# Weight sums of the first FFN moved to the first projection, and the context's gate and up as half-precision pairs

## The chip, the core and the metric

The kernel runs on one core of a Trainium2 chip. The metric is the device time of one execution, in microseconds. Five engines work beside each other, each through its own queue in order: TensorE (PE, with the weight load PEld beside it), VectorE (DVE), ScalarE (ACT), GpSimd (POOL) and SyncE (SP). SP, POOL and ACT can start transfers between HBM and SBUF.

## The reference

Two layers of a backbone over 1024 latent tokens and 256 context tokens, with 1024 channels. Layer 0 mixes with a Fourier part and a Hyena part (long convolutions), layer 1 with neighbourhood attention. Each layer ends with a SwiGLU block, which is what the change is about:

```python
def swiglu(u, w_gate, w_up, w_down):
    return (jax.nn.silu(u @ w_gate) * (u @ w_up)) @ w_down
...
        h_lat = h_lat + g2 * swiglu(modulate(rms_norm(h_lat, norm2_g[i]), sh2, sc2),
                                    ffn_w_gate[i], ffn_w_up[i], ffn_w_down[i])
        if not last:
            h_ctx = h_ctx + cg1 * y_ctx
            h_ctx = h_ctx + cg2 * swiglu(modulate(rms_norm(h_ctx, norm2_g[i]), csh2, csc2),
                                         ffn_w_gate[i], ffn_w_up[i], ffn_w_down[i])
```

The hidden width is 2816, which is 22 blocks of 128 columns; gate and up together are 44 weight tiles of 128 x 1024 floats (512 KB) for each layer. Inputs and outputs are float32.

## The kernel before, in words

**Two numbers for one.** A float32 operand is split into a high and a low part, and a product is three matmuls: high by high, high by low, low by high. There are two kinds of pair. `split` (L285) makes a pair of rounded float32 parts: ScalarE copies the high part (L287), VectorE subtracts (L289). `half_split` (L1215) makes a pair of float16 parts: ScalarE multiplies by a scale and rounds (L1218), VectorE forms the rest (L1219). The float16 pair needs a scale, so that its values fit: for weights it is taken from the sum of absolute values of the tiles (`abs_sums`, L1247; the instruction is on L1251), added over the partitions by a small matmul on TensorE (`over_partitions`, L1294) and inverted on VectorE (`scale_cols`, L1311); for activations it comes from the modulation columns (`operand_scale`, L1221, with an all-reduce on GpSimd). The result of a product is multiplied by the inverse of both scales.

**The stages that matter here, in order.**

- *First projection* (`in_proj`, L779): 16 output blocks over latent and context tokens. For each, ScalarE sums a weight tile three blocks ahead and splits the one of the next block; results are evicted by ScalarE and VectorE. Two generators run beside it, called once per block: the context's filter (`filter_raw`, `filter_spectrum`), whose eight matrices go through `cmat` (L321), and the modulation columns (`ada_group`).
- *First output projection* (`out_proj`, L1178): eight output blocks for the context and the first half of the latent tokens (`pcs` (2, 0)), then `after1`, then eight for the other half. Operands are float32 pairs. A generator, `qkv_sums` (L1253), is called once per block: it loads 44 weight tiles over the GpSimd queue and sums them on ScalarE, three to a call. Four of them are layer 0's first gate and up tiles, 32 are for attention, eight are for layer 1's gate and up.
- `after1` spills the new residual, normalizes the context into float32 pairs (`norm_block`, L537), computes the operand scale and the scales of the four early tiles (`first_scales`, L1269), and begins the latent operands (`wino_first`, L1321).
- *Context's gate and up* (first loop of `ffn`, L1491): for each of 22 blocks, two weight tiles are loaded over SP into an `s4` tile and split into float32 pairs; 48 matmuls of 128x256 follow (`lin`, L338), then Silu on ScalarE (L1529) and a product on VectorE (L1530). The pairs rotate over the tags `wh`, `wl` and, every third time, both buffers of `ws` (`pair3`, L301); the last two blocks use `wh` and `wl` alone.
- *Latent gate and up* (second loop of `ffn`): a Strassen-Winograd scheme on 512-token halves, 11 pairs of blocks, seven products each for gate and up, in float16 pairs (L1449); ScalarE snaps results out of PSUM (L1454). `wino_weights` (L1395) loads two tiles for a key, one into `ws` and one into `s4`, and, where the scale isn't there yet, sums both and makes it (`weight_scale`, L1305).
- Afterwards: the down projections, attention, and layer 1's FFN, which the diff doesn't touch.

**What sets the order.** The program is written against a tile framework. Each tag of a pool has a fixed number of buffers: `ws`, `wh` and `wl` have two each (pool `pw`, 128 x 1024 floats), `s4` has 20. The framework plans a timeline with a cost model at build time: on each engine the ready instruction that stands first in the program goes next, and a tile takes a buffer when one is free. So an instruction can go far ahead of its place in the program, as far as buffers allow; on the chip each engine then keeps that planned order, and waits at an instruction whose operand isn't there. `follow` (L226) ties instructions behind a given one. `ld` starts a transfer from SP, `ldr` from GpSimd, `lda` from ScalarE. `PAD_C` is an unused column block ahead of the constants.

Of the kernel before, what the change touches and what calls it, by code (L numbers as in the profile page):

```python
# [32 lines left out]
PAD_C, PAD_T, SHIFT = 176, 160, 16  # L33
# [168 lines left out]
class Builder:  # L202
# [176 lines left out]
    def weights16(self, src, scale, w=1024, cut=False, load=None):  # L379
        st = self.pw.tile([P, 1024], F32, tag="ws", name=self.nm("ws"))  # L380
        hi, lo = (self.pw.tile([P, 1024], F16, tag=g, name=self.nm(g)) for g in ("wh", "wl"))
        (load or self.ld)(st.rearrange("p (n k) -> p n k", n=4) if cut else st[:, :w], src)
        self.half_split(st[:, :w], scale, hi[:, :w], lo[:, :w])
        return hi, lo
# [830 lines left out]
    def half_split(self, src, scale, hi, lo):  # L1215

        nc = self.nc
        nc.scalar.activation(hi, src, AF.Copy, scale=scale)  # L1218
        nc.vector.scalar_tensor_tensor(lo, src, scale, hi, op0=MUL, op1=SUB)  # L1219
# [33 lines left out]
    def qkv_sums(self):  # L1253

        a = self.a
        self.qs = self.C(44)
        src = [a["wv"][ch, kp] for ch in range(2) for kp in range(4)]
        src += [a[n][b] for n in ("wq", "wk", "w_out2") for b in range(KB)]
        for l, i in ((0, 0), (1, 0), (1, 1)):
            src += [a[n][l, 2 * i + k] for n in ("gate", "up") for k in (0, 1)]  # L1260
        for j, k in enumerate((32, 33, 34, 35, *range(32), *range(36, 44))):
            t = self.S4()
            self.ldr(t, src[k])
            self.abs_sums([t], self.qs[:, k:k + 1])
            if j % 3 == 2:
                yield
        yield

    def first_scales(self, l):  # L1269

        keys = [(l, i, m) for i in range(l + 1) for m in (0, 1)]
        n, k = len(keys), 3 * len(self.wsc)
        q = self.qs[:, 32 + 4 * l:36 + 8 * l]
# [217 lines left out]
    def ffn(self, l, u, h, hs, second, after, keep=None, begun={}):  # L1491
# [28 lines left out]
        if u is not None:  # L1520
            for fb in range(NFB):
                wide = 3 if fb < NFB - 2 else 2
                gh, gl = self.weights(a["gate"][l, fb], wide=wide)
                uh, ul = self.weights(a["up"][l, fb], wide=wide)
# [4 lines left out]
                nc.scalar.activation(t[:, :256], ga[:, :256], AF.Silu)  # L1529
                nc.vector.tensor_tensor(t[:, :256], ua[:, :256], t[:, :256], MUL)  # L1530
# [591 lines left out]
    def run(self):  # L2122
# [100 lines left out]
        self.in_proj(u, ((filt, 1), (ada, 2)))  # L2223
# [59 lines left out]
        def after1(pcs):  # L2283
            spill(h, hs0, pcs)
            if 0 in pcs:
                uf.t.update(self.new_act(pcs=(2,)).t)
                rs = self.rms(pcs)
                for b in range(KB):
                    self.norm_block({b: h.ap(0, b, 2)}, b, 2, 0, 3, uf, rs[0])
                load_h((1,))  # L2290
                self.ucol, self.usi = self.operand_scale(0, 3, (0, 1))
                self.first_scales(0)
# [219 lines left out]
```

## Time and profile before

| | us |
|---|---|
| median of 3 runs | 2919.48 |
| lowest and highest | 2914.33, 2921.39 |
| the profiled execution | 2919.95 |
| its span, first to last instruction | 2918.2 |
| first projection, about | 200 to 405 |
| first output projection, about | 725 to 850 |
| context's gate and up, about | 850 to 981 |
| latent gate and up of layer 0, about | 981 to 1320 |

The profile is of one execution. Its page gives each engine's busy time, a table of 40 slices, the transfer queues, a chain of waits followed back from the end, and groups of instructions: line, engine, operation, output and input names, shape and count, busy time and mean, and then the idle time of the engine just before them with what ended it. In a timeline, a row is the start, the duration, the engine and the line; an idle time before it, and who ended it, stands in brackets. A stage row gives the stretch, its length, the busy time and count of PE, PEld, DVE, ACT and POOL, the granted TensorE clock (1.00 is full), the busy share of the transfer engines, and GB/s. Matmuls are pipelined, so the distance from one start to the next is the cost, not the duration.

### The profile page before, as it was taken

What the parts mean: (1) busy time and instruction counts of PE and PEld (TensorE: products, weight loads), DVE (VectorE), ACT (ScalarE), POOL (GpSimd) and SP (SyncE); (2) the same over time, 40 slices, a digit from 0 to 9 for tenths busy, and PEclk for the clock granted to TensorE, in tenths of its full rate; (3) what the DMA queues carried; (4) which work ended last, traced back from release to release, by engine and by line L of the source; (5) the groups of instructions that cost most, each with busy time, mean ns of one, the idle gap of its engine ahead of it and who ended that gap; (6) DMA issues with size and microseconds to landing.
All of it is one profiled execution on the core that took longest, in us unless ns stands there. A gap on an engine that the chain in (4) does not pass through costs nothing. (4 is left out here: it accounts for less than half of the span.)

```text
span 2918.2 us, 46050 instructions
## 1 busy us (share of the span) xinstructions
PE 2766.6 (95%) x16163; PEld 1714.2 (59%) x16163; DVE 2094.0 (72%) x3833; ACT 1647.7 (56%) x2899; POOL 642.6 (22%) x1057
## 2 busy tenths in 40 slices
PE   6989999999989999999999999999999999999998
PEld 3766557888879644444555844676665444444554
DVE  4778867585467798877886767776676778775765
ACT  4674324454675667654555555676664477654553
POOL 1012013354220121213120012444443022112000
PEclk8989999999999999999999999999999999999999
DMA  6574434358785555566994798777775666424753
GB/s 254 187 265 161 161 122 151 111 168 286 285 344 182 207 205 197 201 213 240 327 333 161 273 337 294 179 188 172 185 198 188 236 226 231 153 93 184 242 191 113
DMA packets 325156, 615.98 MB, mean 211 GB/s; under 512 B 90934, under 2 KB 130552, under 8 KB 324922
## 3 DMA queue, kind: packets, MB, share of 16 engines
q1 hardware_dynamic: 252378, 384.38, 39.9%
q0 software_dynamic: 70240, 224.45, 21.6%
q10 hardware_dynamic: 2304, 4.20, 0.4%
q8 instruction: 127, 2.08, 0.3%
q14 instruction: 107, 0.88, 0.1%
HBM read 455.33 MB, written 135.53 MB: 202 GB/s over the span
## 5 line engine op out<-in xcount | busy, mean ns | idle before, releaser
L1449 PE MATMUL ps<-s,s 128*128 128x512 f16 x2592 | 582.2, 382 | 14.4 <-ACT tk L1454 6.8
L1449 PEld LDWEIGHTS <-s 128*128 128x128 f16 x2640 | 259.0, 98 | 332.6 <-issue 27.8
L283 PE MATMUL ps<-s,wh 128*128 128x256 f32 (+3 forms) x1752 | 398.2, 331 | 11.1 <-ACT wh L287 5.4
L1218 ACT ACTIVATE s<-s,c 128x512 f16<-128x512 f32 (+1 forms) x324 | 233.5, 754 | 141.9 <-DMA s<-d 79.9
L1219 DVE SCALAR_TENSOR_TENSOR s<-s,c,s 128x512 f16<-128x512 f32 (+1 forms) x324 | 247.4, 794 | 84.5 <-ACT s L1218 84.1
L1666 PE MATMUL ps<-s 128*128 128x512 f16 (+2 forms) x1308 | 303.4, 378 | 2.0 <-DVE s L1219 2.0
L283 PE MATMUL pq<-s,wh 128*128 128x512 f16 (+1 forms) x1000 | 280.3, 354 | 9.8 <-DMA wh<-d 5.4
L283 PE MATMUL ps<-s,wl 128*128 128x256 f32 (+3 forms) x876 | 261.6, 331 | 1.3 <-DVE wl L289 1.2
L283 PEld LDWEIGHTS <-wh 128*128 128x128 f16 x1664 | 160.9, 99 | 170.2 <-issue 20.9
L1666 PEld LDWEIGHTS <-s 128*128 128x128 f16 x1536 | 148.5, 98 | 178.9 <-issue 6.5
L274 POOL DMA_DIRECT2D d<-s x201 | 109.0, 543 | 640.5 <-DVE s L1510 178.6
L283 PE MATMUL ps<-s,s 128*128 128x65 f16 (+5 forms) x2666 | 222.3, 236 | 27.5 <-DMA s<-s 11.4
L335 ACT CAST mat<-cs 128x1024 fp32r<-128x1024 f16 (+2 forms) x120 | 111.6, 935 | 140.6 <-PE ps L283 57.3
L283 PEld LDWEIGHTS ps<-s,wh 128*128 128x128 f32 x1088 | 177.5, 192 | 18.1 <-ACT wh L287 5.7
L283 PE MATMUL ps<-s,mat 128*128 128x512 f32 x696 | 184.7, 413 | 3.3 <-DVE s L289 2.9
L1449 PE MATMUL ps<-s,wh 128*128 128x512 f16 x616 | 184.9, 379 | 1.8 <-DVE g L1463 1.4
L283 PE MATMUL pq<-s,wl 128*128 128x512 f16 (+1 forms) x500 | 174.5, 354 | 0.5 <-DMA wl<-d 0.5
L283 PEld LDWEIGHTS <-s 128*128 128x128 f16 x2400 | 114.5, 98 | 82.9 <-DMA s<-s 11.5
L283 PEld LDWEIGHTS ps<-s,mat 128*128 128x128 f32 x696 | 136.5, 199 | 37.9 <-DVE s L289 3.8
L1251 ACT ACTIVATE t<-s 128x1024 bf16<-128x1024 f32 (+1 forms) x164 | 141.9, 867 | 12.2 <-DVE c L470 8.4
L283 PEld LDWEIGHTS ps<-s,s 128*128 128x128 f32 (+1 forms) x746 | 113.6, 192 | 32.1 <-ACT s L287 7.0
L283 PEld LDWEIGHTS <-wl 128*128 128x128 f16 x832 | 82.3, 99 | 77.4 <-issue 4.5
(431 smaller groups left out, 5477.3 us busy)
## 6 DMA issues: line engine op xcount, KB each, us to landing
s<-d SPq DMA_DIRECT2D x294, 256.0 KB, 4.0
d<-s POOLq DMA_DIRECT2D x157, 256.0 KB, 3.2
s<-in_down SPq DMA_DIRECT2D x154, 256.0 KB, 5.4
s<-in_ada_w POOLq DMA_DIRECT2D x48, 512.0 KB, 4.8
g<-in_bias POOLq DMA_DIRECT2D x128, 192.0 KB, 3.6
s<-in_gate SPq DMA_DIRECT2D x46, 512.0 KB, 3.7
s<-in_up SPq DMA_DIRECT2D x46, 512.0 KB, 4.0
d<-g POOLq DMA_DIRECT2D x87, 256.0 KB, 2.9
```

Of the source, the lines that this page charges most:

```text
L274: self.last_ldr = self.nc.gpsimd.dma_start(out, in_).ins
L283: self.nc.tensor.matmul(o, l, r, start=st, stop=sp)
L335: self.nc.scalar.copy(m, st)
L1218: nc.scalar.activation(hi, src, AF.Copy, scale=scale)
L1219: nc.vector.scalar_tensor_tensor(lo, src, scale, hi, op0=MUL, op1=SUB)
L1251: self.nc.scalar.activation(junk[:, :t.shape[1]], t, AF.Abs, scale=2.0 ** -15, accum_out=st[:, k:k + 1])
L1449: nc.tensor.matmul(ps, x[:, sl], y, start=first and j == 0 and x is wh and y is xh, stop=j == 3 and x is wl, skip_group_check=True)
L1666: m = nc.tensor.matmul(acc[j][:, c0:c1], x[:, sl], y[:, xs], start=first and k == 0, stop=last and k == 2, skip_group_check=True)
```

## The change

Four things are changed.

1. **Sums of all 44 gate and up tiles of layer 0 ahead of the FFN.** A new generator `gate_sums` loads 32 of them over ScalarE's own queue into the two `ws` buffers and sums them in place on ScalarE: two loads ahead of the first projection, then two sums, each followed by the next load, at each of its 16 blocks. The other 12 go to the head of `qkv_sums`, which then has 52 tiles: four to a call for the first 16, then three.
2. `first_scales(0)` makes all 22 scales of layer 0 at once, from the new columns `fs`. `wino_weights` then finds every scale of layer 0 and sums nothing. Layer 1 is unchanged.
3. **The context's gate and up use float16 pairs.** The context is normalized after the operand scale is there, with `norm_half` in place of `norm_block`; the weights come from a new function `weights3`, which keeps the rotation over `wh`, `wl` and `ws` for all 22 blocks; the inverse scales go into the Silu and into the product.
4. `PAD_C` falls by 40 columns and `qs` by 4, against 44 columns for `fs`.

```diff
--- before.py
+++ after.py
@@ -30,7 +30,7 @@
 WID = {0: 512, 1: 512, 2: 256, 3: 256, 4: 256}
 OFF = {0: 0, 1: 512, 3: 512, 4: 768}
 KSTART = (0, 8, 24, 32)
-PAD_C, PAD_T, SHIFT = 176, 160, 16
+PAD_C, PAD_T, SHIFT = 136, 160, 16
 BOPS = ("B11", "B21", "T2", "T1", "T3", "B22", "T4")
 
 
@@ -381,6 +381,15 @@
         hi, lo = (self.pw.tile([P, 1024], F16, tag=g, name=self.nm(g)) for g in ("wh", "wl"))
         (load or self.ld)(st.rearrange("p (n k) -> p n k", n=4) if cut else st[:, :w], src)
         self.half_split(st[:, :w], scale, hi[:, :w], lo[:, :w])
+        return hi, lo
+
+    def weights3(self, src, scale):
+        self.p3 = (getattr(self, "p3", 0) + 1) % 3
+        tags = ("ws", "ws") if self.p3 == 0 else ("wh", "wl")
+        st = self.S4()
+        hi, lo = (self.pw.tile([P, 1024], F16, tag=g, name=self.nm(n)) for g, n in zip(tags, ("wh", "wl")))
+        self.ld(st, src)
+        self.half_split(st, scale, hi, lo)
         return hi, lo
 
     def setup(self):
@@ -1216,7 +1225,7 @@
 
         nc = self.nc
         nc.scalar.activation(hi, src, AF.Copy, scale=scale)
-        nc.vector.scalar_tensor_tensor(lo, src, scale, hi, op0=MUL, op1=SUB)
+        self.last_lo = nc.vector.scalar_tensor_tensor(lo, src, scale, hi, op0=MUL, op1=SUB).ins
 
     def operand_scale(self, l, m, conds):
 
@@ -1253,24 +1262,48 @@
     def qkv_sums(self):
 
         a = self.a
-        self.qs = self.C(44)
+        self.qs = self.C(40)
         src = [a["wv"][ch, kp] for ch in range(2) for kp in range(4)]
         src += [a[n][b] for n in ("wq", "wk", "w_out2") for b in range(KB)]
-        for l, i in ((0, 0), (1, 0), (1, 1)):
-            src += [a[n][l, 2 * i + k] for n in ("gate", "up") for k in (0, 1)]
-        for j, k in enumerate((32, 33, 34, 35, *range(32), *range(36, 44))):
+        src += [a[n][1, 2 * i + k] for i in (0, 1) for n in ("gate", "up") for k in (0, 1)]
+        todo = [(a[("gate", "up")[j // 2 % 2]][0, j // 4 * 2 + j % 2], self.fs[:, j:j + 1])
+                for j in range(32, 4 * (NFB // 2))]
+        todo += [(x, self.qs[:, k:k + 1]) for k, x in enumerate(src)]
+        for j, (x, col) in enumerate(todo):
             t = self.S4()
-            self.ldr(t, src[k])
-            self.abs_sums([t], self.qs[:, k:k + 1])
-            if j % 3 == 2:
+            self.ldr(t, x)
+            self.abs_sums([t], col)
+            if j % 4 == 3 if j < 16 else j % 3 == 0:
                 yield
         yield
 
+    def gate_sums(self):
+
+        nc, a = self.nc, self.a
+        n = 32
+        self.fs = self.C(4 * (NFB // 2))
+        tiles = {}
+
+        def load(j):
+            if j < n:
+                t = tiles[j] = self.pw.tile([P, 1024], F32, tag="ws", name=self.nm("ws"))
+                self.lda(t, a[("gate", "up")[j // 2 % 2]][0, j // 4 * 2 + j % 2])
+
+        load(0)
+        load(1)
+        yield
+        for j in range(n):
+            t = tiles.pop(j)
+            nc.scalar.activation(t, t, AF.Abs, scale=2.0 ** -15, accum_out=self.fs[:, j:j + 1])
+            load(j + 2)
+            if j % 2:
+                yield
+
     def first_scales(self, l):
 
-        keys = [(l, i, m) for i in range(l + 1) for m in (0, 1)]
+        keys = [(l, i, m) for i in range(2 if l else NFB // 2) for m in (0, 1)]
         n, k = len(keys), 3 * len(self.wsc)
-        q = self.qs[:, 32 + 4 * l:36 + 8 * l]
+        q = self.qs[:, 32:40] if l else self.fs
         s, inv = self.scale_cols(q, self.wcol, k, n)
         for j, key in enumerate(keys):
             self.wsc[key] = (s[:, j:j + 1], inv[:, j:j + 1])
@@ -1519,15 +1552,15 @@
             self.pad(self.pt, PAD_T)
         if u is not None:
             for fb in range(NFB):
-                wide = 3 if fb < NFB - 2 else 2
-                gh, gl = self.weights(a["gate"][l, fb], wide=wide)
-                uh, ul = self.weights(a["up"][l, fb], wide=wide)
+                (gs, gi), (us, ui) = (self.wsc[(l, fb // 2, m)] for m in (0, 1))
+                gh, gl = self.weights3(a["gate"][l, fb], gs)
+                uh, ul = self.weights3(a["up"][l, fb], us)
                 lo = self.last_lo
                 ga = self.lin(gh, gl, 0, range(KB), u, (2,))[2]
                 ua = self.lin(uh, ul, 0, range(KB), u, (2,))[2]
                 t = self.T()
-                nc.scalar.activation(t[:, :256], ga[:, :256], AF.Silu)
-                nc.vector.tensor_tensor(t[:, :256], ua[:, :256], t[:, :256], MUL)
+                nc.scalar.activation(t[:, :256], ga[:, :256], AF.Silu, scale=gi)
+                nc.vector.scalar_tensor_tensor(t[:, :256], ua[:, :256], ui, t[:, :256], op0=MUL, op1=MUL)
                 self.ldr(hidc[fb // 2][:, fb % 2], t[:, :256])
                 if fb >= 2:
                     with self.follow(last):
@@ -2220,7 +2253,11 @@
                             self.filter_spectrum("c", 1, raws["c"][1])) for x in g)
         for i in range(8):
             self.tap(f"u{i}", u.ap(0, i, 0))
-        self.in_proj(u, ((filt, 1), (ada, 2)))
+        gsum = self.gate_sums()
+        next(gsum)
+        self.in_proj(u, ((filt, 1), (ada, 2), (gsum, 1)))
+        for _ in gsum:
+            pass
         drain(ada)
         for _ in filt:
             pass
@@ -2283,12 +2320,13 @@
         def after1(pcs):
             spill(h, hs0, pcs)
             if 0 in pcs:
-                uf.t.update(self.new_act(pcs=(2,)).t)
                 rs = self.rms(pcs)
-                for b in range(KB):
-                    self.norm_block({b: h.ap(0, b, 2)}, b, 2, 0, 3, uf, rs[0])
                 load_h((1,))
                 self.ucol, self.usi = self.operand_scale(0, 3, (0, 1))
+                for b in range(KB):
+                    if b % 2 == 0:
+                        self.new_half(uf, ((b, 2), (b + 1, 2)))
+                    self.norm_half(h.ap(0, b, 2), b, 2, uf, rs[0], self.ucol)
                 self.first_scales(0)
                 for _ in self.wino_first(h, 0, 3, rs[1]):
                     pass
```

## The prediction

> **What bounds the kernel now.** I read the page's sums first, then the table of stages, then the waits of TensorE stage by stage.
>
> ```profile
> span 2918.2 us, 46050 instructions
> PE 2766.6 (95%) x16163; PEld 1714.2 (59%) x16163; DVE 2094.0 (72%) x3833; ACT 1647.7 (56%) x2899; POOL 642.6 (22%) x1057
> ```
> ```profile
> core 0: us, PE busy (x) PEld busy (x) DVE busy (x) ACT busy (x) POOL busy (x), PEclk, DMA share, GB/s
> 200.00:405.00 205.00, 193.12 (x1057) 111.30 (x1057) 152.53 (x317) 80.47 (x149) 31.21 (x36) 0.95 0.49 179
> 725.00:850.00 125.00, 119.42 (x602) 100.44 (x600) 64.01 (x103) 83.36 (x148) 31.97 (x60) 0.97 0.76 297
> 850.00:990.00 140.00, 132.90 (x1092) 127.46 (x1093) 100.87 (x128) 81.80 (x119) 13.00 (x24) 0.96 0.63 230
> ```
> The four stages that the change touches are the first projection (200 to 405), the first output projection (725 to 850), the context's gate and up (850 to 981) and the latent gate and up (981 to 1320). TensorE is the bound in all of them. So work taken from ScalarE is worth only the TensorE idle time that it ends, and the clock lost after such idle time:
>
> ```profile
> 993.20:996.60 3.40, 3.02 (x8) 1.09 (x8) 3.40 (x7) 3.05 (x9) 0.00 (x0) 0.50 0.87 330
> 1276.50:1279.90 3.40, 3.29 (x8) 1.13 (x8) 3.40 (x7) 3.34 (x9) 0.54 (x1) 0.50 0.45 154
> 1020.00:1260.00 240.00, 239.53 (x1121) 108.65 (x1120) 210.28 (x379) 158.20 (x305) 47.66 (x88) 1.00 0.57 205
> ```
> From 1020 to 1260 TensorE is busy 239.5 of 240 us at full clock: there is nothing to gain there, although most of the weight sums run there. Each of the two stretches at clock 0.50 loses half of 3.4, or 1.7 us.
>
> **The change part by part.**
>
> *Half-precision pairs in the context.* 22 blocks of 48 matmuls, 1056 of 128x256, change from f32 to f16.
> ```profile
> 881.00:967.00 86.00, 86.00 (x761) 86.00 (x760) 64.81 (x82) 47.39 (x67) 8.67 (x16) 1.00 0.51 180
> ```
> ```profile
> 1822.11 0.38 PE L283 MATMUL pq<-s,wh 128*128 128x256 f16 x2
> ...
> 1823.75 0.38 PE L283 MATMUL pq<-s,wh 128*128 128x256 f16 x2
> ```
> Undisturbed, 761 f32 matmuls take 86.0 us, 113.0 ns each. The f16 form stands in attention: five groups of three begin 1.64 us apart, 109.3 ns each. Gain: 1056 x 3.7 ns = 3.9 us, and no more, although the weight load gets shorter: the matmul itself sets the pace. ScalarE and VectorE stay covered, with 67 of 86 us and less for both. The scaled split is dearer by 0.1 us on either, as these rows of the next stage against the split of today show:
> ```profile
> 978.46 1.15 ACT L1218 ACTIVATE wh<-ws,c 128x1024 f16<-128x1024 f32 x1 [1.67 <-PE ps L283]
> ```
> ```profile
> 979.90 1.28 DVE L1219 SCALAR_TENSOR_TENSOR wl<-ws,c,wh 128x1024 f16<-128x1024 f32 x1
> ```
> ```profile
> L287 ACT CAST wh<-s 128x1024 fp32r<-128x1024 f32 x44 | 45.8, 1048 | 40.6 <-issue 26.4 <-PE ps L283 13.4 <-DMA s<-in_up 0.8
> L289 DVE TENSOR_TENSOR wl<-s,wh 128x1024 fp32r<-128x1024 f32 x44 | 53.7, 1225 | 31.6 <-ACT wh L287 31.6
> ```
> The scale must be there first: its last sums are the first 12 of the output projection, and the operand scale comes before the second half of it, with eight blocks of TensorE work still between it and the first context matmul. I cost that order at nothing.
>
> *Sums gone from the latent gate and up.* 40 sums leave ScalarE (22 keys of two tiles, less the two keys summed ahead today), 20 scale chains leave VectorE, 20 one-column matmuls leave TensorE. What ends late there now:
> ```profile
> L1449 PE MATMUL ps<-s,s 128*128 128x512 f16 x1056 | 238.2, 382 | 8.2 <-ACT g L1454 4.2 <-ACT tk L1454 4.0
> ```
> ```profile
> 993.58 4.24 PE L1449 MATMUL ps<-s,s 128*128 128x512 f16 x12 [2.87 <-ACT g L1454]
> ...
> 1276.61 4.37 PE L1449 MATMUL ps<-s,s 128*128 128x512 f16 x12 [2.91 <-ACT tk L1454]
> ```
> ```profile
> 989.05 1.04 ACT L1251 ACTIVATE t<-ws 128x1024 bf16<-128x1024 f32 x1
> ...
> 991.92 1.04 ACT L1251 ACTIVATE t<-s 128x1024 bf16<-128x1024 f32 x1
> 992.87 0.19 ACT L1251 ACTIVATION_READ_ACCUMULATOR t<-s 128x1 f32 x1
> 992.96 0.57 ACT L1454 COPY g<-ps 128x512 f32<-128x512 f32 x1
> ```
> ```profile
> 1271.46 1.05 ACT L1251 ACTIVATE t<-ws 128x1024 bf16<-128x1024 f32 x1
> ...
> 1274.95 1.05 ACT L1251 ACTIVATE t<-s 128x1024 bf16<-128x1024 f32 x1
> ```
> A sum holds ScalarE from 991.92 to 992.96, 1.04 us with its read. Before either late copy stand two weight sums. Without them the copy comes 2.1 us earlier and the stall falls from 2.9 to 0.8, twice: 4.2 us. I take both stretches at half clock as gone with them, 3.4 us (below: none). The small matmuls cost 0.03 us each between their neighbours (997.65 to 997.68):
> ```profile
> 997.65 0.17 PE L283 MATMUL ps<-st,c 128*128 128x1 bf16 x1
> 997.68 0.59 PE L1449 MATMUL ps<-s,wh 128*128 128x512 f16 x2
> ```
> That is 0.6 us. What is late next in both places is the half-precision splitting on ScalarE, which stays.
>
> The Trainium skill, "TensorE: Matmul & The Clock Gate" (what's actually happening), has the clock set by a free-running window of some 3.4 us; the 3.40 us rows agree in length. By that rule a shorter stall in the wrong phase can still cost a window, and the sum would be 3.4 us higher, 2916 (estimate from the 1.7 us above).
>
> *32 sums in the first projection.* Each adds 1.04 us on ScalarE and one issue on its queue:
> ```profile
> L271 ACTq DMA_DIRECT2D d<-s x16: 326/326/1475, 1451.8 to 1606.3; - x16
> ```
> 32 x (1.04 + 0.33) = 44 us on top of 80.5 in 205 us. An output block has 205 / 16 = 12.8 us there, so ScalarE's 8 us per block have cover. Behind a sum that waits for its load stand the evictions, the weight halves and the context filter's casts, in order. The 16.8 MB add 82 GB/s to 179. Only the opening has no cover: TensorE waits 5.6 us for the first scale, behind a chain of ScalarE work that shows no idle bracket from 199.88 to 204.48.
> ```profile
> 203.81 0.16 PE L283 MATMUL pq<-st,c 128*128 128x2 bf16 x1 [5.63 <-DVE st L1300]
> ```
> ```profile
> 199.88 0.64 ACT L451 ACTIVATE s<-s 128x512 f32<-128x512 f32 x1
> ...
> 204.48 1.15 ACT L1218 ACTIVATE wh<-s,c 128x1024 f16<-128x1024 f32 x1
> ```
> Two issues there are 0.65 us; one hoisted sum would be 1.04 more; nothing if they are issued in an earlier gap. I take 1.0.
>
> The Trainium skill, "DMA: Bandwidth & Descriptors" (Issuing engines are not separate DMA queues), says that transfers started by different engines share the same 16 DMA engines. No run so far shows the two queues together there. The transfers are at 395 GB/s at that place (window 200 to 207):
> ```profile
> DMA packets 1315, 2.76 MB, mean 395 GB/s; under 512 B 149, under 2 KB 277, under 8 KB 1314
> ```
> By that rule the first two loads (1.05 MB) hold up the projection's weights at its saturated start, and 1.0 would be 2.5, the sum 2914 (estimate).
>
> *Staging tiles.* The loads use the two `ws` buffers, which the context filter's eight matrices use too. Program order makes them alternate, so the sums cannot run far ahead. Nothing, as TensorE has the projection's matmuls meanwhile.
>
> *52 loads for 44 in the output projection.* Four more fall in its second half, where DMA is full (window 816 to 872):
> ```profile
> DMA packets 6177, 22.37 MB, mean 399 GB/s; under 512 B 727, under 2 KB 727, under 8 KB 6171
> ...
> s<-in_gate SPq DMA_DIRECT2D x9, 512.0 KB, 13.5
> ```
> ```profile
> 851.46 0.79 PE L283 MATMUL ps<-s,wh 128*128 128x256 f32 x2 [2.33 <-ACT wh L287]
> ...
> 874.94 0.50 PE L283 MATMUL ps<-s,wh 128*128 128x256 f32 x2 [3.07 <-ACT wh L287]
> ```
> 2.1 MB at 399 GB/s are 5.3 us. They go ahead of the context's first weights, which land 13.5 us after issue. Bounds: nothing, if today's two waits are ScalarE's alone; 5.3 plus 4 sums x 1.04, 9.5 us, if all of it reaches TensorE. I take half of the transfer, 2.6.
>
> *Hand-over to the latent part.* Today the last two blocks leave `ws` free and the latent gate's first load goes at 967.6:
> ```profile
> L268 SPq DMA_DIRECT2D ws<-in_gate x20: 327/328/328, 967.6 to 2588.4; - x20
> ```
> ```profile
> ws<-in_gate SPq DMA_DIRECT2D x20, 512.0 KB, 4.3
> ```
> Now the 42nd of 44 pairs takes both `ws` buffers until one block (48 x 109.3 ns, 5.2 us) before the end. Load 4.3 us (the median landing of this tile), then 1.15 and 1.28 for the halves: 6.7 us against 5.2, so 1.4 us late.
>
> *Sum against the profiled execution* (2919.95 us, span 2918.2): -3.9 -4.2 -3.4 -0.6 +1.0 +2.6 +1.4 = -7.1, so 2912.8; say **2913**. The median of the runs, 2919.48, is 0.5 lower, so it is no other case.
>
> **The rivals.**
> 1. *The context's opening is cleaned too.*
> ```profile
> 849.80:856.70 6.90, 4.78 (x20) 4.49 (x21) 3.59 (x3) 5.69 (x9) 0.00 (x0) 0.51 1.02 419
> ```
> The order on every engine is planned anew, and its two waits (2.33 and 3.07 us) with the stretch of 6.9 us at clock 0.51 after the first cost some 8.8 us. Against it: DMA is fuller there. If they go and nothing is paid there (-8.8 -2.6): 2901.
> 2. *The opening takes the whole bound.* 9.5 for 2.6, with one more stretch at half clock (1.7): 2921. For it: the saturated rows above.
> 3. *Slower: ScalarE stands at the head of its queue for loads that land late.*
> ```profile
> s<-in_ada_w SPq DMA_DIRECT2D x26, 512.0 KB, 4.3
> ```
> With two buffers, a load issued after one sum has only the other sum (1.04 + 0.33) before it is wanted, and a 512 KB load of this stage lands in 4.3 us (median); 2.5 to 3 us of standing for a pair. It decides where a cast of the context filter (8 matrices, woven into TensorE's order) stands behind it: 8 x 2.5 = 20 us, 2933. It needs loads placed too early by the planner; against it, ScalarE idles more than half of this stage, and a wait inside a gap costs nothing.
> 4. *The pairs don't do what they say:* the f16 spacing isn't reached because the splits feed it too slowly. 3.9 us less gain: 2917.
>
> **How the numbers follow.** Forecast (2905 to 2918): 0.42. Rival 1: 0.20; rival 2: 0.13; rival 3: 0.17; rival 4: 0.08. A measurement of this kernel tells about 0.3%, 8.8 us, from no change: faster is below 2910.7, slower above 2928.2. Faster: rival 1 and 0.18 of the forecast's lower end, 0.38. Slower: rival 3 and 0.04 of rival 2, 0.21. The rest, 0.41, is within. The range 2898 to 2932 reaches over rivals 1, 2 and 4 and the near part of 3; the likeliest's own is 2905 to 2918.
>
> **What would show it.** Context rows at 109 ns for a matmul; no copy (L1454) waited for over 1 us around 993 and 1276, and no half clock there; TensorE's waits between 205 and 405 for ScalarE casts (rival 3); its waits in the first 25 us of the context (rivals 1 and 2); a wait of 1 to 2 us at the first latent product. The prediction is wrong if TensorE's idle time in the first projection grows by over 5 us, or if the later layers, which the change doesn't touch, shift by more than 3 us.

## The result, and the profile after

The changed kernel is slightly slower: 2923.78 us median (20 runs, 2914.30 to 2932.64) beside 2913.79 us for the kernel before on the same chip (20 runs, 2905.21 to 2925.07). The ratio is 1.0029, 95% interval 1.0019 to 1.004, so +8.5 us by the ratio (the medians lie 10.0 us apart). The forecast was 2913, that is 7.1 us below the profiled execution of before: the sum missed by some 16 us, and in direction. The profiled execution took 2921.78 us; that of before, 2919.95 us, lay some 6 us above its median, so the two traces show a difference of 1.8 us where the runs show 8.5.

The page of the changed kernel, its span and its engines:

```profile
span 2920.0 us, 45967 instructions
PE 2762.0 (95%) x16143; PEld 1692.6 (58%) x16143; DVE 2092.4 (72%) x3753; ACT 1653.6 (57%) x2899; POOL 644.9 (22%) x1065
```

Busy times and shares are nearly those of before: the work was only moved. Its stages, in the columns of the stage rows of before (length, PE, PEld, DVE, ACT, POOL, clock, DMA share, GB/s):

```profile
200.00:405.00 205.00, 182.40 (x991) 106.04 (x991) 141.94 (x297) 108.34 (x203) 29.46 (x34) 0.93 0.67 230
725.00:850.00 125.00, 118.02 (x588) 98.85 (x589) 66.64 (x116) 83.31 (x152) 34.11 (x64) 0.96 0.80 304
850.00:990.00 140.00, 130.68 (x1057) 112.31 (x1056) 95.42 (x115) 90.84 (x128) 16.70 (x31) 0.95 0.69 251
900.00:970.00 70.00, 70.00 (x644) 62.74 (x642) 59.75 (x73) 44.37 (x57) 7.49 (x14) 1.00 0.57 192
990.00:1390.00 400.00, 395.54 (x1867) 182.18 (x1866) 334.29 (x534) 215.08 (x396) 85.57 (x159) 1.00 0.61 216
```

In the first row TensorE is busy 182.4 of 205 us, where it was 193.1: the first projection pays. The last row has the latent stage at full clock. The row from 900 to 970, which lies inside the context, reads before:

```profile
900.00:970.00 70.00, 70.00 (x620) 70.00 (x620) 50.05 (x62) 38.74 (x55) 7.05 (x13) 1.00 0.52 180
```

Where the lag arises is read from four marks, each the first row of a line in either trace: Hyena's first transposes, the output projection's first update, the first latent product, the first down product. Before, then after:

```profile
459.69 0.71 PE L867 MATMUL ps<-c,s 128*128 128x128 f32 x5
730.31 0.48 DVE L1197 SCALAR_TENSOR_TENSOR s<-ps,c,s 128x256 f32<-128x256 f32 x1 [1.76 <-PE ps L283]
981.10 0.60 PE L1449 MATMUL ps<-s,wh 128*128 128x512 f16 x2
1381.98 0.38 PE L1666 MATMUL ps<-s 128*128 128x512 f16 x1
```

```profile
471.50 0.71 PE L876 MATMUL ps<-c,s 128*128 128x128 f32 x5
743.39 0.48 DVE L1206 SCALAR_TENSOR_TENSOR s<-ps,c,s 128x256 f32<-128x256 f32 x1 [1.77 <-PE ps L283]
998.50 0.39 PE L1482 MATMUL ps<-s,wh 128*128 128x512 f16 x1 [0.76 <-ACT wh L1227]
1388.83 0.38 PE L1699 MATMUL ps<-s 128*128 128x512 f16 x1
```

So the first projection costs 11.8 us; output projection and context together, 250.8 us before, take 255.1; the latent gate and up falls from 400.9 to 390.3. The first mark shows also that the projection ends near 460, not at 405 as I had taken it.

The rest, from the first down product to the end of the span, takes 1531.2 us where it took 1536.2, although the diff does not touch that code. ScalarE runs the same instructions there in another order, since the planner lays out the whole program anew. Without these 5.0 us the traces would differ by some 7 us.

**The first projection.** The opening, on TensorE and on ScalarE:

```profile
206.54 0.16 PE L283 MATMUL pq<-st,c 128*128 128x2 bf16 x1 [14.01 <-DVE st L1333]
208.43 0.39 PE L283 MATMUL pq<-s,wh 128*128 128x256 f16 x1 [1.73 <-ACT wh L1227]
```
```profile
197.11 1.06 ACT L1297 ACTIVATE ws<-ws 128x1024 f32<-128x1024 f32 x1 [2.50 <-DMA ws<-in_up]
...
203.09 1.05 ACT L1297 ACTIVATE ws<-ws 128x1024 f32<-128x1024 f32 x1
...
207.24 1.14 ACT L1227 ACTIVATE wh<-s,c 128x1024 f16<-128x1024 f32 x1
```

The planner has put early sums (L1297) into the chain that leads to the first scale. One waits 2.50 us for its load, another stands in front of the three sums that the scale needs, and the first weight half starts at 207.24, where before it started at 204.48. TensorE stands 14.01 us, where it stood 5.63. The tile view of `ws` between 200 and 472 sums what follows:

```profile
its engine sat idle before it (us, times) until:
  DMA ws<-in_up: 26.7, 12
  DMA ws<-in_gate: 18.4, 10
who waited for it (us, times):
  ACT ws L1297: 45.1, 22
busy tenths in 40 slices 0000120000000000000000000000000000000000
DMA to landing us min/median/max: 3.2/4.5/7.0
```

ScalarE stood 45.1 us in front of sums whose tile had not landed, 22 times. This is how one of them reaches TensorE:

```profile
387.19 1.06 ACT L1297 ACTIVATE ws<-ws 128x1024 f32<-128x1024 f32 x1 [1.61 <-DMA ws<-in_up]
...
388.25 1.13 ACT L1227 ACTIVATE wh<-s,c 128x1024 f16<-128x1024 f32 x1
```
```profile
389.43 0.82 PE L283 MATMUL ps<-s,wh 128*128 128x256 f16 x2 [5.74 <-ACT wh L1227]
```

The weight half is queued behind this sum, the last of four that wait for their loads one after another (2.88, 2.06, 1.35 and 1.61 us), and TensorE waits 5.74 us for the half.

**The output projection.** From its first to its last update it takes 126.6 us for 115.6 before. The first 16 of the 24 updates take 62.4 us in both traces, so all 11.0 us arise in the second half, 64.1 us for 53.1. ScalarE and TensorE shortly before its end:

```profile
859.12 0.63 ACT L505 ACTIVATE tk<-s 128x512 f32<-128x512 f32 x1 [2.90 <-DVE s L1206]
859.65 1.04 ACT L1260 ACTIVATE t<-s 128x1024 bf16<-128x1024 f32 x1
860.60 0.19 ACT L1260 ACTIVATION_READ_ACCUMULATOR t<-s 128x1 f32 x1
860.69 1.03 ACT L287 CAST wh<-ws 128x1024 fp32r<-128x1024 f32 x1
```
```profile
861.77 0.74 PE L283 MATMUL ps<-s,wh 128*128 128x512 f32 x2 [3.48 <-ACT wh L287]
```

The cast of the next weights stands behind a square that waits for the update of TensorE's own result, and behind a sum. TensorE waits 3.48 us for it.

### The profile page after: what moved, and what is told of

Same layout as the page of the kernel before. It is cut to its first block, busy times and chain, and to the rows that moved or that the text cites. A ratio compares the mean times of both kernels' runs of the same rounds, so it can differ in the third digit from the quotient of the medians.

```text
span 2920.0 us, 45967 instructions
## 1 busy us (share of the span) xinstructions
PE 2762.0 (95%) x16143; PEld 1692.6 (58%) x16143; DVE 2092.4 (72%) x3753; ACT 1653.6 (57%) x2899; POOL 644.9 (22%) x1065
## 5 line engine op out<-in xcount | busy, mean ns | idle before, releaser
L1482 PE MATMUL ps<-s,s 128*128 128x512 f16 x2064 | 464.2, 379 | 5.3 <-ACT g L1487 3.2
L283 PE MATMUL ps<-s,wh 128*128 128x256 f16 (+3 forms) x1752 | 396.4, 331 | 15.8 <-ACT wh L1227 9.9
L283 PEld LDWEIGHTS <-wh 128*128 128x128 f16 x2368 | 231.2, 99 | 194.1 <-ACT wh L1227 27.8
L283 PE MATMUL ps<-s,wl 128*128 128x256 f16 (+3 forms) x876 | 261.0, 331 | 0.5 <-DVE wl L289 0.5
L283 PEld LDWEIGHTS <-wl 128*128 128x128 f16 x1184 | 117.6, 99 | 82.2 <-issue 6.0
L1260 ACT ACTIVATE t<-s 128x1024 bf16<-128x1024 f32 (+1 forms) x152 | 129.0, 849 | 38.3 <-DMA s<-in_down 19.6
L1482 PE MATMUL pq<-s,s 128*128 128x512 f16 x576 | 132.8, 380 | 0.3 <-ACT s L1227 0.2
```

What stands on the lines that cost most here:

```text
L283: self.nc.tensor.matmul(o, l, r, start=st, stop=sp)
L1260: self.nc.scalar.activation(junk[:, :t.shape[1]], t, AF.Abs, scale=2.0 ** -15, accum_out=st[:, k:k + 1])
L1482: nc.tensor.matmul(ps, x[:, sl], y, start=first and j == 0 and x is wh and y is xh, stop=j == 3 and x is wl, skip_group_check=True)
```

## The experiments

Each was timed against the kernel before. One thousandth of the ratio is 2.9 us. The ratios come from several chips, on which the median of the kernel before lies between 2913.79 and 2919.02 us. The marks are of one profiled execution each, and those lie up to 6 us from the median of their kernel (13 in e8_hyena8), so a verdict rests on the ratio, and on a mark only where several kernels agree. The last column is the time from the first down product to the end, in code that no edit touches.

| kernel | first transposes | output projection and context | latent gate and up | ratio to before, 95% | rest |
|---|---|---|---|---|---|
| before | 459.7 | 250.8 | 400.9 | 1 | 1536.2 |
| after | 471.5 | 255.1 | 390.3 | 1.0029 (1.0019 to 1.004) | 1531.2 |
| e1_follow | 463.0 | 255.5 | 389.6 | 1.0001 (0.9987 to 1.0014) | 1542.5 |
| e7_sync_queue | 473.4 | 256.7 | 389.6 | 1.0043 (1.0025 to 1.006) | 1534.4 |
| e2_nosums | 455.9 | 250.1 | 390.8 | 0.9943 (0.9922 to 0.9965) | 1538.1 |
| e9_loads32 | 454.3 | 248.3 | 396.6 | 0.9977 (0.9961 to 0.9993) | 1532.7 |
| e4_late8 | 471.4 | 240.2 | 396.8 | 0.9995 (0.9978 to 1.0011) | 1532.9 |
| e5_both | 460.2 | 239.7 | 395.5 | 0.9971 (0.9957 to 0.9984) | 1542.4 |
| e12_pace44 | 463.6 | 249.6 | 393.7 | 0.9997 (0.9983 to 1.0012) | 1539.4 |
| e10_loads8 | 464.2 | 249.0 | 394.8 | 1.0031 (1.0015 to 1.0047) | 1543.9 |
| e11_sums8 | 461.4 | 256.4 | 393.3 | 1.0034 (1.0019 to 1.0048) | 1535.0 |
| e13_order52 | 460.0 | 255.4 | 389.7 | 1.0003 (0.9987 to 1.0019) | 1538.0 |
| e15_square52 | 461.2 | 254.9 | 390.4 | 1.0004 (0.9986 to 1.0022) | 1541.2 |
| e6_f32ctx | 461.7 | 251.3 | 394.6 | 0.9994 (0.9982 to 1.0006) | 1531.6 |
| e8_hyena8 | 458.9 | 239.2 | 389.9 | 0.9974 (0.9957 to 0.9992) | 1530.2 |
| e14_order44 | 462.5 | 239.0 | 390.3 | 0.9978 (0.9964 to 0.9992) | 1530.3 |
| e17_best | 459.5 | 239.7 | 389.5 | 0.9955 (0.994 to 0.997) | 1530.2 |

### The first projection

**e1_follow**: the same sums and loads, each tied behind a weight half.

```diff
-            nc.scalar.activation(t, t, AF.Abs, scale=2.0 ** -15, accum_out=self.fs[:, j:j + 1])
-            load(j + 2)
+            with self.follow(self.last_half):
+                nc.scalar.activation(t, t, AF.Abs, scale=2.0 ** -15, accum_out=self.fs[:, j:j + 1])
+                load(j + 2)
```

> The 32 early sums stay in the first projection, but each sum, and the load that follows it, now goes out right behind a weight half on ScalarE, so none can be planned far ahead and a load has most of an output block (12.8 us) to land before it is wanted. Same bytes, same number of instructions. Theory A (ScalarE stands in order behind a sum whose load has not landed): the waits for ws at L1297 fall from 48 us to under 10, TensorE's waits after 210 us in the first projection from 15.4 to about 8, the first transpose of the Hyena stage comes at 460 to 463 instead of 471.5, and the time falls by 9 to 12 us against the kernel after (2912 to 2915). Theory B (the 16.8 MB on the shared DMA engines delay the projection's weights): nothing changes by more than 3 us. Theory C (44 us of added ScalarE work, whatever its place, delays the halves): nothing changes by more than 3 us either, and TensorE goes on waiting for wh.

The ratio falls from 1.0029 to 1.0001, some 8 us and a little less than expected, and the first transposes come 8.5 us earlier. The opening and the `ws` tiles of this kernel:

```profile
203.67 0.16 PE L283 MATMUL pq<-st,c 128*128 128x2 bf16 x1 [7.55 <-DVE st L1334]
```
```profile
  ACT ws L1298: 5.2, 6
...
DMA to landing us min/median/max: 3.2/4.4/7.4
```

45.1 us of standing (48 in the expectation, counted from 170 on) become 5.2, while the loads land as before (4.4 us, median, beside 4.5). Theory A holds: of these 8 us neither the transfer nor the amount of work is the cause, but the sum's place in ScalarE's order. One number missed: TensorE's named waits after 210 us still add up to 15.4 us, only in smaller pieces; it is its busy time between 212 and 456 that rose, from 228.6 to 231.9, and the opening that shrank by 6.5.

**e7_sync_queue**: the changed kernel with `self.ld` for `self.lda` in `gate_sums`.

> The changed kernel with the 32 early loads issued by SyncE instead of ScalarE's own queue, sums as they were. ScalarE no longer spends 0.33 us on each issue (11 us in all, most of it beside TensorE's work). If standing for loads is the cost, the queue does not matter: within 4 us of the changed kernel. If the cost is ScalarE's queue: 6 to 10 us below it. Rival: a load now stands at the head of SyncE's queue until its buffer is free, and the projection's own weights behind it: slower than the changed kernel by over 4 us.

1.0043, whose interval overlaps that of the changed kernel, and the same late mark, 473.4. The queue was not the cost.

**e2_nosums**: no sum and no early load of layer 0's gate and up anywhere, a constant for them; the other 40 sums go three to a call.

```diff
-        todo = [(a[("gate", "up")[j // 2 % 2]][0, j // 4 * 2 + j % 2], self.fs[:, j:j + 1])
-                for j in range(32, 4 * (NFB // 2))]
+        todo = []
...
+        nc.vector.memset(self.fs, 2.0 ** -11)
```

> Left out: all 44 weight sums of the first layer's gate and up with their 44 loads; a constant stands in their place, so the scales are constants (the scale chains stay). The output projection then has 40 loads. If the change's costs all come from these sums in their two new places, what is left is its gain alone: 17 us below the kernel before (2897 to 2900), first transpose of the Hyena stage at 457 to 460, first latent product at 975 to 978. If the context's new form or the new planning order costs as well, less than 12 us below the kernel before.

0.9943, which is 16.6 us below the kernel before: the gain without its price, and with four loads fewer in the output projection than before.

**e9_loads32**: e5_both (below) with the 32 early loads, but not their sums, for which constants stand.

```diff
-            t = tiles.pop(j)
             with self.follow(self.last_half):
-                nc.scalar.activation(t, t, AF.Abs, scale=2.0 ** -15, accum_out=self.fs[:, j:j + 1])
                 load(j + 2)
```

> e5_both with the 32 loads of the first projection but without their 32 sums (constants in their place, so those scales are constants): the 16.8 MB alone, without 33 us of ScalarE. The first transpose of the Hyena stage comes at 460.2 in e5_both and at 455.9 without loads and sums. If the transfers are what the early sums still cost: 459 to 462 here, and the time within 2 us of e5_both. If ScalarE's work is: 455 to 457, and 3 to 5 us below e5_both.

In the two traces, e9_loads32 first and e2_nosums second, the first transposes stand at:

```profile
454.33 0.49 PE L876 MATMUL ps<-c,s 128*128 128x128 f32 x3
```
```profile
455.86 0.49 PE L876 MATMUL ps<-c,s 128*128 128x128 f32 x3
```

With all 16.8 MB and no sum the mark is no later than with neither. So the transfers are covered, and what the well placed sums still cost, 3 to 10 us by the marks of the kernels that place them so (458.9 to 464.2; 5.9 us by e5_both, from which this kernel differs by the sums alone), goes with ScalarE's part in them, its work and what standing is left. The time did not follow (0.9977 beside 0.9971): this kernel lost it in the output projection, whose code is that of e5_both, 248.3 us for 239.7.

### The output projection

**e4_late8**: layer 1's eight sums go to the latent gate and up, three sums a step for the other 44.

```diff
+        self.late_sums = [todo.pop() for _ in range(8)]
...
-            if j % 4 == 3 if j < 16 else j % 3 == 0:
+            if j % 3 == 2:
...
+            if l == 0 and self.late_sums:
+                x, col = self.late_sums.pop()
+                t = self.S4()
+                self.ldr(t, x)
+                self.abs_sums([t], col)
```

> Eight of the sums in the output projection (layer 1's, which are wanted last) go back into the latent gate and up, one for each block there, so the output projection has 44 loads as before the change. Theory D (eight more loads and sums in a stage whose DMA is full): the stage from the Hyena's end to its last product is 7 to 11 us shorter, the latent stage loses 0 to 2, and the time falls by 5 to 10 us against the kernel after (2914 to 2919). Rival E (the stage is longer because the order on each engine was planned anew, or because it begins later): within 3 us of the kernel after.

**e5_both**: e1_follow and e4_late8 together.

> Both edits together: early sums behind weight halves, eight sums moved from the output projection to the latent gate and up. If A and D both hold their costs add, 14 to 20 us below the kernel after (2904 to 2910), which is also 4 to 10 below the kernel before. If only A holds: 9 to 12 below the kernel after. If neither: within 3 us of it.

e4_late8 is 10 us below the changed kernel, e5_both 17 (0.9971): the two costs are separate and add, and e5_both lies below both kernels. Output projection and context fall from 255 to 240 us in both; eight sums back in the latent stage cost about 6 us there (395.5 beside 389.6 in e1_follow, 396.8 beside 390.3 in the changed kernel).

What in those eight is dear? Three controls on e5_both: **e12_pace44**, its 44 at the pace of the 52; **e10_loads8**, that and eight loads that nothing reads; **e11_sums8**, that and eight sums over a tile already there.

```diff
-            if j % 3 == 2:
+            if j % 4 == 3 if j < 16 else j % 3 == 0:
```
```diff
+            else:
+                self.ldr(self.S4(), x)
```
```diff
+            else:
+                self.abs_sums([t], junk[:, j - 44:j - 43])
```

> Control for e10_loads8 and e11_sums8: e5_both with the 44 loads and sums of its output projection at their pace (four a step for the first 16, then three) instead of three a step throughout. If the pace, not the eight extra, made those two 17 and 18 us slower: 10 us or more slower than e5_both. If the eight extra did: within 3 us of e5_both.

> As e5_both, with eight loads of 512 KB that nothing reads added behind the 44 in the output projection, so it has the 52 transfers of the changed kernel, and its pace, without eight of its sums. Hyena's end to the first latent product took 513.3 us in e5_both and 526.5 with all 52 sums. If the transfers are the cost (4.2 MB at about 400 GB/s are 10.5 us): 6 to 11 us slower than e5_both. If ScalarE's work or its order is: within 3 us of it.

> As e5_both, with eight sums over a tile that is already there added behind the 44 in the output projection: 52 sums, 44 transfers, the changed kernel's pace; their results are not used. If ScalarE's added 8.3 us, or its place in front of the weight casts, is the cost: 5 to 11 us slower than e5_both. If the transfers are: within 3 us of it. If neither this nor the loads alone costs anything, it is the sum waiting for its own load that costs.

The pace alone takes back 7.6 us of time (0.9997), and 9.9 us of the stretch (249.6 for 239.7) without one load or sum more. On top of it e10_loads8 is 9.9 us slower and e11_sums8 10.8. But both together are no dearer than either: e1_follow, which has them, stands at 1.0001 without the late sums. So neither answer of mine was right: no single resource has a price for eight more. Nor do the traces put the 9.9 us of the unread loads into the output projection: the stretch of e10_loads8, 249.0, is that of e12_pace44, 249.6, and its rest is the longest of all. The trace of e11_sums8 shows the other form of the wait:

```profile
860.63 1.06 ACT L1260 ACTIVATE t<-s 128x1024 bf16<-128x1024 f32 x1 [2.81 <-DMA s<-in_w_out]
861.60 0.19 ACT L1260 ACTIVATION_READ_ACCUMULATOR t<-s 128x1 f32 x1
861.69 1.03 ACT L287 CAST wh<-ws 128x1024 fp32r<-128x1024 f32 x1
```
```profile
862.77 1.46 PE L283 MATMUL ps<-s,wh 128*128 128x512 f32 x3 [8.80 <-ACT wh L287]
```

Here the cast is held by a sum that waits for its load, and TensorE stands 8.80 us. The eight extra sums are not the reason: e12_pace44, which hasn't got them, has nearly the same wait.

```profile
857.43 1.67 PE L283 MATMUL ps<-s,wh 128*128 128x512 f32 x4 [8.58 <-ACT wh L287]
```

**e13_order52** and **e15_square52** try to mend the order with all 52 in place: sums only behind the next weight cast, then squares too.

```diff
+            with self.follow(self.last_hi):
+                self.abs_sums([t], col)
```
```diff
+                    with self.follow(self.last_hi):
+                        self.square(t, nb, pc)
```

> The early sums behind weight halves (as in e1_follow) and all 52 loads and sums in the output projection, but each of those sums may go out only behind the float32 cast of the next block's weights on ScalarE. No byte and no instruction less than in e1_follow. If the output projection pays because weight casts stand behind sums and squares in ScalarE's order: TensorE's waits there for wh at L287 (2.4 and 3.5 us, with two half-clock windows of 1.7) go, and the time is 5 to 11 us below e1_follow, that is 5 to 11 below the kernel before. If the stage has simply 4.2 MB or 8.3 us of ScalarE too much: within 3 us of e1_follow, the waits only change their place.

> e13_order52 (early sums behind weight halves, 52 loads and sums in the output projection) with one rule more: the square of an updated block (L505 on ScalarE) may also go out only behind the cast of the next block's weights. In e13_order52 the last cast ran at 850.68 behind a square that had waited 2.70 us for the block's update until 849.11, although its weights were issued at 837.4 and land in 7.0 us. If this order, and not the 4.2 MB or the 8.3 us of ScalarE, is what the output projection pays: the 3.48 us wait for wh and its half-clock window go, Hyena's end to the first latent product falls from 529 to 518 to 522, and the time is 5 to 10 us below e13_order52. If the volume is the cost: within 3 us of e13_order52.

Both stay where e1_follow is (1.0003 and 1.0004). In e13_order52 the wait of 3.48 us for the cast is still there. In e15_square52 it is gone, but an earlier one for a cast has grown from 2.10 to 3.44 us (at 823.67), and so has the wait for the squares at the end, 2.23 us in e13_order52:

```profile
858.02 0.59 PE L283 MATMUL pq<-c,tk 128*128 128x1 f32 x2 [3.78 <-DVE tk L510]
```
```profile
855.58 1.06 ACT L1261 ACTIVATE t<-s 128x1024 bf16<-128x1024 f32 x1 [1.40 <-DMA s<-in_up]
...
856.63 0.61 ACT L505 ACTIVATE tk<-s 128x512 f32<-128x512 f32 x1
```

The square is late behind a sum that waits, and TensorE waits for the squares. So these two rules of order give nothing back, and my theory of the order is not shown for this stage. Five kernels with 52 take 254.9 to 256.7 us for this stretch, five with 44 at three a step 239.0 to 240.2. But e9_loads32 with 44 at three a step takes 248.3, and e2_nosums with 40, 250.1, with a wait of 6.77 us for a cast. The first 16 updates take 62.3 to 62.4 us in every kernel, so the output projection's own differences all arise in its second half: 53.1 us in the kernel before, 64.1 in the changed one, 66.8 in e2_nosums with the fewest loads. What decides it stays open; the number of loads and sums alone does not.

### The context, and the best version

**e6_f32ctx**: e5_both with float32 pairs in the context again.

```diff
-                gh, gl = self.weights3(a["gate"][l, fb], gs)
-                uh, ul = self.weights3(a["up"][l, fb], us)
+                wide = 3 if fb < NFB - 2 else 2
+                gh, gl = self.weights(a["gate"][l, fb], wide=wide)
+                uh, ul = self.weights(a["up"][l, fb], wide=wide)
```

> The version with both edits (e5_both), but with the context's gate and up in float32 pairs as before the change: one part of the change undone where nothing else disturbs it. In the trace 70 us of the context hold 620 matmuls in float32 and 644 in half precision, 4.2 ns a matmul, so 1056 of them should cost 4.5 us: 4 to 6 us slower than e5_both. Rival: the half-precision form also moves the order on ScalarE, and undoing it costs under 2 us or over 8.

0.9994 for 0.9971, 6.7 us slower; the stretch grows by 11.7. The page of before had two waits in the context's opening, and they are back in e6_f32ctx:

```profile
855.97 0.58 PE L283 MATMUL ps<-s,wh 128*128 128x256 f32 x1 [3.13 <-ACT wh L287]
```
```profile
879.29 0.38 PE L283 MATMUL ps<-s,wh 128*128 128x256 f32 x1 [3.05 <-ACT wh L287]
```

In e5_both the longest wait at that place is this one:

```profile
858.44 0.28 PE L283 MATMUL ps<-s,wl 128*128 128x256 f16 x1 [0.93 <-DVE wl L1228]
```

So by the trace the half-precision pairs are worth the pace of their matmuls, 4.5 us, and in this order also the two waits; the time shows 6.7 us in all.

**e8_hyena8** puts the eight sums into the Hyena stage (`gate_sums` goes on to 40, two at every second step there), **e14_order44** adds the rule of e13_order52 to it, **e17_best** that of e15_square52.

> As e5_both, but layer 1's eight sums go to the Hyena stage, behind the 32 in the same two buffers, instead of the latent gate and up. From the first latent product to the first down product e5_both takes 395.4 us, the kernel without the early sums 390.8. If the eight sums are dear in the latent stage because ScalarE is what comes late there: that stretch falls to 389 to 391, the Hyena stage (ScalarE busy about half of the time, DMA share 0.57) grows by under 2, and the time is 3 to 6 us below e5_both. If the Hyena stage has no room for them: the same time as e5_both within 2 us.

> e8_hyena8 (early sums behind weight halves, layer 1's eight in the Hyena stage, 44 in the output projection) with the same rule that a sum goes out behind the next block's weight cast. e8_hyena8 has only one wait of over 1 us left there, so this should gain 0 to 4 us on it: 7 to 12 us below the kernel before. Rival: the rule makes sums late, and the operand scales that need them hold up the context: slower than e8_hyena8 by over 3 us.

> e14_order44 (early sums behind weight halves, layer 1's eight in the Hyena stage, 44 in the output projection behind casts) with the squares behind the casts as well: all that helped, together. e14_order44 has no wait for a float32 cast left in its profile, so the rule has little to gain there: 6 to 12 us below the kernel before, within 3 us of e14_order44. More than 12 below would mean that the order still cost where the profile of e14_order44 did not show it.

The latent stage gets its 5 to 6 us back in all three (389.5 to 390.3). e8_hyena8 and e14_order44 are nevertheless no faster than e5_both (0.9974, 0.9978). From the first transposes to the first update e14_order44 takes 281.5 us and e17_best 280.8, the kernels without sums there 270.3 to 277.1, so those two pay for the eight sums in the Hyena stage; e8_hyena8, with 275.7, doesn't show it. e17_best reaches 0.9955, 13.1 us below the kernel before; its interval overlaps those of e5_both, e8_hyena8 and e14_order44, so it is the best seen, not shown to be the best. Nor is its lead seen where its rule acts: its stretch of output projection and context is 239.7 us, and its first down product starts at 1369.54, that of e5_both at 1369.04. Against the changed kernel, by the two ratios, it is 0.9926.

## Why the prediction was wrong

**The gains were right, and somewhat small.** The pace of the matmuls was 3.7 ns each, 3.9 us; the rows of 70 us hold 644 for 620, so 4.2 ns, 4.5 us. The latent stage was put at 8.2 us; the marks give 10.6 (400.9 to 390.3). The waits for late copies are shorter. These are the same 1260 latent products of layer 0's stage (981 to 1382 before, 998 to 1390 after), with the idle time ahead of them and what ended it in the last part:

```profile
L1449 PE MATMUL ps<-s,s 128*128 128x512 f16 x1260 | 283.8, 382 | 8.2 <-ACT g L1454 4.2 <-ACT tk L1454 4.0
```
```profile
L1482 PE MATMUL ps<-s,s 128*128 128x512 f16 x1260 | 280.6, 379 | 3.7 <-ACT g L1487 3.2 <-ACT s L1227 0.5
```

Two waits of over 1 us for a copy are left, 1.46 us at 1068.20 and 1.41 us at 1269.20, where the sum had two of 0.8. No half-clock stretch is left: the row from 990 to 1390 has 1.00. The prediction had taken from the free-running window of the Trainium skill, "TensorE: Matmul & The Clock Gate" (what's actually happening), that a shorter stall can still cost a window, 2916 in place of 2913; these two cost none. The hand-over, 1.4 us, measures 0.76 in the row at 998.50.

**The failed step is "32 sums in the first projection", with "Staging tiles": cover for 8 us of ScalarE in a block, 1.0 us for the opening, and "the sums cannot run far ahead".** I added up busy time and left out standing time. ScalarE's work of 33 us was covered but for the 3 to 10 us that even well placed sums cost; the 45.1 us that it stood for loads were not in the sum, because I trusted two buffers to keep the sums near their place. They kept them near each other. The opening paid 2.7 us (first matmul at 208.43 for 205.69), the blocks after it 9.1, in all 11.8 for 1.0. e1_follow shows the cause: same bytes, same instructions, another order, 8 us less. Rival 3 had this mechanism, sized at 20 us and tied to the filter's casts; what stands behind the sums are weight halves and copies out of PSUM (TensorE waits 7.9 and 3.9 us for them after 210), and the price is about 10. My argument against it, that ScalarE idles more than half of the stage, is the error in short: an idle share says nothing about who stands in front of whom.

The sign that I had named for a wrong prediction, TensorE's idle time in this stage up by over 5 us, is what the trace shows: 22.6 us for 11.9 in the row from 200 to 405. The other sign, a shift of the later layers by more than 3 us, shows too, 5.0 us. But that part of the trace lies between 1530.2 and 1543.9 us in the 17 kernels, so its cause stays open; the sum had no term for it.

The Trainium skill, "DMA: Bandwidth & Descriptors" (Issuing engines are not separate DMA queues), made me name a rival price for the transfers, 1.5 us more. The two marks of e9_loads32 and e2_nosums show none, and in e7_sync_queue another issuing engine brings no gain (1.0043 beside 1.0029), which agrees with that section.

**The second failed step is "52 loads for 44": 2.6 of a bound of 9.5.** The output projection took 11.0 us longer, all of it in the second half, where I had looked for it; that is near the size of rival 2, which had transfers taken by TensorE. The step failed in what it priced. I counted bytes and put the new pace of the calls at nothing, but e12_pace44 pays 7.6 us for the pace with no byte more, and e2_nosums, with four loads fewer than before, has a longer second half than the changed kernel. What TensorE waits for there are weight casts and squares in ScalarE's order, 3.48 and 3.38 us in the changed kernel. Which instructions make them late is not shown: the rules of e13_order52 and e15_square52 only moved such waits and gained nothing.

**Rival 1 came true only in part.** It put the context's two waits and their half clock at 8.8 us. In the changed kernel the two waits for casts are down to one of 1.29 us, but the wait for the squares ahead of them is 3.38 us, and there are still 10.2 us at half clock at that place. Where the output projection is light, in e5_both, the waits and the half clock there are gone, and undoing the pairs in e6_f32ctx brings them back: without the 4.5 us of the matmuls that costs 7.2 us by the stretch and 2.2 by the time.

That 2923.78 lies within 2898 to 2932 is no merit of the sum: that range reaches over the rivals, and the prediction's own range for its mechanism ended at 2918.

Rival 4, that the half-precision spacing is not reached, did not happen: 644 matmuls in 70 us are 108.7 ns each.

## What to carry to other kernels

Work moved to an engine with spare time is free only if its operands are there when its turn comes: count what stands behind each moved instruction, and how long its load takes, before counting shares of busy time. Where a planner hoists, tie the moved work behind an instruction that must go first, and look at the waits of the tile that it reads. In a stage that already runs near its limit on two sides, the price of more work could not be read from its bytes or its busy time here, and the pace at which the work is handed out counted too. So measure such a stage first with the moved work left out, and look at more than one order before you name a cause.

## What the hardware showed unasked

A wait can be dearer than its own length. After the 3.48 us wait at 861.77 in the changed kernel, and around the next one at 873.28, the clock was halved:

```profile
862.90:866.30 3.40, 3.27 (x8) 2.62 (x9) 0.08 (x1) 2.99 (x6) 1.08 (x2) 0.50 1.02 418
866.30:873.10 6.80, 3.60 (x16) 2.61 (x14) 1.31 (x2) 3.42 (x6) 0.55 (x1) 1.00 1.03 421
873.10:879.90 6.80, 6.62 (x32) 5.18 (x33) 2.88 (x4) 4.05 (x8) 0.00 (x0) 0.50 1.02 418
```

10.2 us at half clock are 5.1 us lost, beside the waits themselves. Not every wait has this price: after those of 1.46 and 1.41 us in the latent stage the clock stayed full. One kernel varies with the clock too: twelve runs of e8_hyena8 lie between 2889.79 us, at a mean clock of 0.985, and 2914.64 us, at 0.979. A single run of such a kernel says little about 10 us.
